# A hybrid decoder layer on one Trainium2 core: rounding each weight tile in a second, casting DMA

## The chip, the core and the metric

The kernel runs on one core of one Trainium2 chip. A core has five engines that work from queues of their own, each strictly in its order: TensorE (PE, matrix products; its weight loads are listed as PEld), VectorE (DVE), ScalarE (ACT), GpSimd (POOL) and SyncE (SP). They meet only through semaphores. Transfers between the chip's main memory and the on-chip memory are done by DMA engines; an instruction on SP or on POOL issues a transfer, and a semaphore tells when it has landed. The metric is the device time of one execution in microseconds (us). The kernel before took 613.98 us, the median of three runs that lie between 613.79 and 614.02.

## The reference

One decoder layer over 1024 tokens of width 1024, float32 throughout. Cut to what matters here:

```python
h = _rmsnorm(x, g_in[l])
proj = h @ w_in[l]                                   # 1024 x 3584
q_sb, k_sb, v_sb, u_c, b_c, c_c, q_mem, gate = jnp.split(proj, SPLIT_POINTS, axis=-1)
y_sb   = _stick_breaking_attention(q_sb, k_sb, v_sb)  # 8 heads of 64
y_conv = b_c * _causal_depthwise_conv(c_c * u_c, conv_w[l], conv_b[l])
mk, mv = jnp.split(_rmsnorm(mem, g_mem[l]) @ w_mem_kv[l], 2, axis=-1)
y_mem  = _memory_attention(q_mem, mk, mv)             # 4 heads of 64, 256 memory tokens
y = jnp.concatenate([_rmsnorm(y_sb), _rmsnorm(y_conv), _rmsnorm(y_mem)], axis=-1)
x = x + (y * jax.nn.silu(gate)) @ w_out[l]
return _rmsnorm(x, g_final)
```

In stick-breaking attention the weight of key s for query t is sigmoid(z_ts) times the product of (1 - sigmoid(z_tj)) over the keys j between s and t; the kernel computes these products as a running scan along the keys.

## The kernel before, in words

**Float32 from float32r.** A product of two float32 matrices is done as three TensorE passes on operands of type float32r. Each operand is split into hi, the value rounded to float32r, and lo, the exact rest: hi*hi + hi*lo + lo*hi. Each weight tile therefore needs three buffers: `raw` as loaded, `hi` and `lo`.

**Stages.** First the normalised input is split (`xh`, `xl`, eight tiles of each) and the values v are computed while the input still arrives. Then 24 tiles of the input projection (128 columns each, 512 KB) and four tiles of the memory's key and value weights (512 KB) are worked off one after the other by `proj`, `mem_kv` and, for the last one, `proj_last`. The order of these 28 is the string `BG`. A generator mixes them with the attention of twelve heads: the scores (z), two sigmoids on ACT (`F`, `sg`), the scan on DVE (lines 399 and 401), a product of `sg` and `F` on DVE or POOL (line 404, by the letters of `MENG`), transposes on TensorE, a split of the transposed weights (hi on ACT, line 341; lo on DVE, lines 342 and 344), and the product with v. POOL also sets the first column of each `F` tile (line 395) and adds up halves of y (line 361). Last comes the output projection: eight weight tiles of 512 KB, eight blocks of 128 rows, and the final norm.

**Weights.** `load_w` loads a tile on SP's queue into `wraw`, of which there is one buffer, rounds it in two halves to `whi` on ACT or DVE (by the 28 letters of `WENG`; lines 142 and 144), and subtracts on POOL to get `wlo` (line 145). There are two buffers each of `whi` and `wlo`: a tile can be made when the tile two before it has had its last matmul. `next_w` asks for a tile's successor as soon as the tile itself is taken into use. The output weights (`woh`, `wol`, lines 764 to 775) use the 16 buffers that `xh` and `xl` held, which fall free one after the other while `proj_last` runs; their rounding is on ACT (line 773), their subtraction on POOL for odd and on DVE for even tiles (line 774). Of their raw tiles `wor` there are three buffers.

**What sets the order.** The program is written through a scheduler that puts the instructions of each engine in an order by its own estimates of time. An edit at one place can thus move instructions everywhere. Once built, the order on each engine is fixed, and an instruction that waits holds up all that stand behind it on that engine. In the listings below, the buffer numbers are those of the built program.

Of the kernel before, what the change touches and what calls it, by code (L numbers as in the profile page):

```python
"""Hybrid decoder layer: stick-breaking attention, short gated convolution and memory
cross-attention heads side by side, group norms, SiLU gate, output projection.

The sequence is processed in reversed order (row j holds token T-1-j), so that the keys of a
query lie after it and the stick-breaking products are forward scans along the free axis:
  state[m] = max(state[m-1] * sigmoid(-z[m-1]), M[m]),   w[m] = sigmoid(z[m]) * state[m],
where M is one at the first key of the row and zero elsewhere.

Float32 products run as float32r passes: each operand is hi + lo, hi = the value rounded to
float32r, lo = the exact rest, and hi*hi + hi*lo + lo*hi carries float32's accuracy.  # L10
"""
# [16 lines left out]
T = 1024  # L28
# [16 lines left out]
# s, v, p: the engine (scalar, vector, pool) that rounds each weight tile, that takes each  # L45
# head's last product of the scan, and that splits its keys
WENG = 'vssssvvvsvvssvvsvvvssvvvvsss'
# [6 lines left out]
def hymba_kernel(ctx, tc, xT, xr, wp, wv, memT, memr, wmem, cols, eye, wout, gfin, out):  # L54
    nc = tc.nc
# [74 lines left out]
    nload = [0]  # L130

    def load_w(src, shape):
        hi = wring.tile(shape, F32R, tag="whi", name=nm("whi"))
        lo = wring.tile(shape, F32R, tag="wlo", name=nm("wlo"))
        raw = wring.tile(shape, F32, tag="wraw", name=nm("wraw"), bufs=1)
        nc.sync.dma_start(out=raw, in_=src)
        n = shape[1] // 2
        onact = WENG[nload[0]] == "s"
        nload[0] += 1
        for c in (slice(0, n), slice(n, 2 * n)):  # L140
            if onact:
                nc.scalar.copy(hi[:, c], raw[:, c])  # L142
            else:
                nc.vector.tensor_copy(hi[:, c], raw[:, c])  # L144
            nc.gpsimd.tensor_tensor(lo[:, c], raw[:, c], f(hi[:, c]), op=ALU.subtract)  # L145
        return hi, lo

# [11 lines left out]
    # the tensor engine's clock comes up on work: zeros, while the first rows load  # L159
# [82 lines left out]
    def behind_attention(ins):  # L242
        # order alone: keeps this work from running out ahead of the attention's steps
        if len(marks) > SLACK:
            tc.add_manual_dep(ins.ins, marks[-1 - SLACK].ins.name,
                              mybir.DependencyInfo(mybir.DependencyClass.NoSync, mybir.DependencyReason.DATA),
                              reason="pace")
# [3 lines left out]
    def proj_last(evac, need):  # L251
        # the input's tiles are done with one after the other: the output's weights take them
        wh, wl = next_w()
        ps = [z_tile(), z_tile()]
        for k in range(KC):
            for n, hf in enumerate(HALVES):
                for a, (ww, xx) in enumerate(((wh, xh), (wh, xl), (wl, xh))):
                    ins = nc.tensor.matmul(ps[n], lhsT=ww[:, k, :], rhs=xx[k][:, hf],
                                           start=(k == 0 and a == 0), stop=(k == KC - 1 and a == 2))
                    if a == 0:  # L260
                        behind_attention(ins)
            yield 1.3
        yield from after(need)
        for n, hf in enumerate(HALVES):
            evac(ps[n], hf)
# [65 lines left out]
    def transposed(blocks):  # L331
        # 4 [query, key] blocks: hi and lo of them; of a third and last one, lo comes after hi
# [21 lines left out]
    def put_own_key(y, av, a, t0):  # L354
        # one block of queries times their own keys: w's hi, then its lo
# [7 lines left out]
    def interleave(first, second):  # L363
        # steps of two lists of (cost, function), in proportion
# [89 lines left out]
    def stats_sum(st, g, first):  # L454
        # sums over the partitions, as a row, which a DMA lays out as [token, block]
        part = small.tile([P, TB], F32, tag="part", name=nm("part"), bufs=2)
        for n, (hi, lo) in enumerate(st["sq"]):
# [3 lines left out]
            row = stage()  # L461
# [8 lines left out]
    def group_stats(c):  # L470
        # the sums of squares of two tiles of 128 columns, a while later
# [222 lines left out]
    def attention(units):  # L694
        # steps of all heads in a row: the scores of a stage run one stage ahead of their use
# [16 lines left out]
    def run(steps, bg, ratio):  # L712
        # attention steps, with the other work in proportion
# [52 lines left out]
    for n, c in enumerate(order):  # L766
        hi = xpool.tile([P, D], F32R, tag="X", name=nm("woh"))
        lo = xpool.tile([P, D], F32R, tag="X", name=nm("wol"))
        raw = post.tile([P, D], F32, tag="wor", name=nm("wor"), bufs=3)
        nc.sync.dma_start(out=raw, in_=wout[c])  # L770
        eng = nc.gpsimd if n % 2 else nc.vector
        for hf in HALVES:
            nc.scalar.copy(hi[:, hf], raw[:, hf])
            eng.tensor_tensor(lo[:, hf], raw[:, hf], f(hi[:, hf]), op=ALU.subtract)  # L774
# [4 lines left out]
    for j in range(TB):  # L779
# [10 lines left out]
        # the last rows end on half a bank: less is left to do after the last product  # L790
# [78 lines left out]
```

## Time and profile before

| | |
|---|---|
| median of three runs | 613.98 us |
| profiled execution: its own time, and the span from its first to its last instruction | 614.2 us, 614.2 us |
| PE busy | 565.8 us, 92% |
| DVE busy | 454.3 us, 74% |
| ACT busy | 350.9 us, 57% |
| POOL busy | 338.7 us, 55% |
| moved by DMA | 48.36 MB, 79 GB/s on average |

A line of a timeline gives the start, the duration, the engine, the line of the kernel, the operation, what it writes and reads, the shapes and the count, and in brackets the idle time of that engine before it and what ended that. A line of a table of groups ends with the busy time of the group, the mean duration of one in ns, and the idle time before them by what ended it. A matmul's duration includes its way through the array; consecutive matmuls start closer together than they last, so a busy PE is not PE at its peak. The profile has no transfer issued by POOL in it: all 22,144 packets of the program's own transfers went through SP's queue.

### The profile page before, as it was taken

The numbers are of one execution on the slowest core, as the hardware profiler recorded it, in microseconds if no ns is written. First come the engines' busy times: TensorE is split into PE (matmuls) and PEld (weight loads), VectorE is DVE, ScalarE is ACT, GpSimd is POOL, SyncE is SP. The second block draws the span as 40 slices with busy tenths as digits, with TensorE's granted clock in tenths as the row PEclk, the third lists the DMA queues.
The fourth block names the chain that finished last, engine by engine and source line by source line (L and its number), as shares of the span: only waits on it lengthen the run. The fifth ranks groups of instructions, "written<-read, shape, count | busy, mean of one in ns | idle before, by whom it ended". The sixth has DMA issues, their size and how long they took to land.

```text
span 614.2 us, 8410 instructions
## 1 busy us (share of the span) xinstructions
PE 565.8 (92%) x2744; PEld 461.6 (75%) x2744; DVE 454.3 (74%) x744; ACT 350.9 (57%) x775; POOL 338.7 (55%) x381
## 2 busy tenths in 40 slices
PE   9999989979899899877979999899988999899995
PEld 5888878758678688755768888778667886688884
DVE  3425159989999996579966766998779668977664
ACT  5646556536685777765745988563645554443232
POOL 2551787454247448987858657448789668411001
PEclk9999999979999999898979999899999999999998
DMA  8931520211302021121313212111011163131311
GB/s 283 403 107 36 137 67 16 57 36 35 104 34 67 5 68 35 34 56 70 98 53 104 70 35 69 34 36 35 4 32 35 35 240 103 69 138 68 114 59 69
DMA packets 22188, 48.36 MB, mean 79 GB/s; under 512 B 7808, under 2 KB 8320, under 8 KB 22144
## 3 DMA queue, kind: packets, MB, share of 16 engines
q1 hardware_dynamic: 22144, 47.82, 24.3%
q8 instruction: 22, 0.36, 0.2%
q14 instruction: 22, 0.18, 0.1%
HBM read 36.78 MB, written 4.20 MB: 67 GB/s over the span
## 4 chain that ended last, share of the span: by engine, by line
DVE 17%; PE 16%; ACT 7%; issue 7%; POOL 6%; DMA 2%; POOLq 0%; DVEq 0%; ACTq 0%
PE tr L802 6%; PE pj L273 3%; PE pj L802 3%; PE z L802 2%; DVE wtl L342 2%; ACT e L546 2%; DVE F L401 2%; DVE F L399 2%; POOL wlo L145 2%; DMA wor<-in_wout 1%; DVE whi L144 1%; POOL sg L404 1%; DVE wol L774 1%; DVE mx L542 1%; DVE y L352 1%
## 5 line engine op out<-in xcount | busy, mean ns | idle before, releaser
L273 PE MATMUL pj<-xh,whi 128*128 128x512 f32 x368 | 150.1, 408 | 4.1 <-DVE mv L681 3.4
L273 PE MATMUL pj<-xl,whi 128*128 128x512 f32 x368 | 146.5, 398 | 0.0
L273 PE MATMUL pj<-xh,wlo 128*128 128x512 f32 x368 | 146.1, 397 | 0.0
L145 POOL TENSOR_TENSOR wlo<-wraw,whi 128x512 fp32r<-128x512 f32 x56 | 81.5, 1469 | 16.2 <-ACT whi L142 11.0
L399 DVE TENSOR_TENSOR_SCAN F<-F,mask 128x513 f32<-128x513 f32 (+2 forms) x64 | 78.8, 1231 | 13.7 <-ACT F L396 11.0
L273 PEld LDWEIGHTS pj<-xh,whi 128*128 128x128 f32 x368 | 70.8, 192 | 17.2 <-DVE mv L681 3.6
L273 PEld LDWEIGHTS pj<-xh,wlo 128*128 128x128 f32 x368 | 70.5, 192 | 14.3
L273 PEld LDWEIGHTS pj<-xl,whi 128*128 128x128 f32 x368 | 70.7, 192 | 12.2
L396 ACT ACTIVATE F<-z,nrq 128x512 f32<-128x512 f32 (+3 forms) x96 | 55.8, 583 | 22.8 <-PE z L389 11.0
L404 POOL TENSOR_TENSOR sg<-sg,F 128x512 f32<-128x512 f32 (+3 forms) x48 | 56.0, 1171 | 20.1 <-DVE F L401 10.3
L342 DVE TENSOR_TENSOR wtl<-tr,wth 128x512 fp32r<-128x512 f32 (+1 forms) x96 | 56.1, 592 | 11.0 <-ACT wth L341 10.1
L361 POOL TENSOR_TENSOR y<-y,avt 64x128 f32<-64x128 f32 x64 | 47.5, 743 | 22.8 <-DVE avt L359 20.1
L341 ACT CAST wth<-tr 128x512 fp32r<-128x512 f32 (+1 forms) x96 | 51.1, 553 | 14.3 <-PE tr L335 12.7
L397 ACT ACTIVATE sg<-z,rq 128x512 f32<-128x512 f32 (+2 forms) x96 | 55.4, 580 | 3.0 <-PE tr L335 2.8
L335 PE MATMUL tr<-ident,sg 128*128 128x128 f32 x288 | 48.4, 285 | 5.6 <-DVE stg L462 2.0
L401 DVE TENSOR_TENSOR_SCAN F<-F,F,mask 128x512 f32<-128x512 f32 (+1 forms) x32 | 43.9, 1371 | 7.6 <-ACT F L396 7.0
L395 POOL MEMSET F<- 128x1 f32 x96 | 8.9, 97 | 72.0 <-DVE F L401 35.8
L814 POOL TENSOR_TENSOR ssf<-ssf,nhalf 128x1 f32<-128x1 f32 x8 | 7.4, 924 | 71.4 <-DVE ssf L811 62.1
L316 POOL TENSOR_TENSOR qs<-qk,q 64x512 fp32r<-64x512 f32 x24 | 32.9, 1377 | 23.9 <-ACT q L315 23.2
L335 PEld LDWEIGHTS tr<-ident,sg 128*128 128x128 f32 x288 | 35.7, 147 | 10.6 <-DVE sg L404 3.1
L429 PE MATMUL av<-wtl,vh 128*128 128x256 f32 x128 | 35.5, 295 | 7.6 <-DVE wtl L342 7.4
L389 PE MATMUL z<-k,q 128*128 128x512 f32 (+2 forms) x96 | 36.2, 377 | 3.1 <-ACT sg L397 2.9
(188 smaller groups left out, 1283.2 us busy)
## 6 DMA issues: line engine op xcount, KB each, us to landing
wraw<-in_wp SPq DMA_DIRECT2D x24, 512.0 KB, 3.3
xs<-in_xr SPq DMA_DIRECT2D x8, 512.0 KB, 8.6
wor<-in_wout SPq DMA_DIRECT2D x8, 512.0 KB, 5.3
acc<-in_xr SPq DMA_DIRECT2D x8, 512.0 KB, 3.4
out<-acc SPq DMA_DIRECT2D x16, 256.0 KB, 2.1
xs<-in_xT SPq DMA_DIRECT2D x7, 512.0 KB, 8.0
qs<-q SPq DMA_DIRECT2D x12, 256.0 KB, 2.9
q<-qs SPq DMA_DIRECT2D x12, 256.0 KB, 2.9
```

Source lines behind the costliest of these rows:

```text
L145: nc.gpsimd.tensor_tensor(lo[:, c], raw[:, c], f(hi[:, c]), op=ALU.subtract)
L273: ins = nc.tensor.matmul(ps, lhsT=ww[:, k, :], rhs=xx[k][:, hf], start=(k == 0 and a == 0), stop=(k == KC - 1 and a == 2))
L335: ins = nc.tensor.transpose(tr[:, i * P : (i + 1) * P], blk, ident)
L341: nc.scalar.copy(wh[:, 0:n], tr[:, 0:n])
L342: nc.vector.tensor_tensor(wl[:, 0:m], tr[:, 0:m], f(wh[:, 0:m]), op=ALU.subtract)
L361: nc.gpsimd.tensor_tensor(y[own, t0 : t0 + P], y[own, t0 : t0 + P], c, op=ALU.add)
L396: nc.scalar.activation(F[:, 1:m], zz[:, 0 : m - 1], AF.Sigmoid, scale=nrq[:, i : i + 1])
L397: nc.scalar.activation(sg[:, c0:c1], zz, AF.Sigmoid, scale=rq[:, i : i + 1])
L399: nc.vector.tensor_tensor_scan(F[:, 0:m], F[:, 0:m], M[:, 0:m], 0.0, ALU.mult, ALU.max)
L401: nc.vector.tensor_tensor_scan(F[:, 0:m], F[:, 0:m], M[:, 130 : 130 + m], prev[:, H - lo : H - lo + 1], ALU.mult, ALU.max)
L404: eng.tensor_tensor(sg[:, c0:c1], sg[:, c0:c1], F[:, 0:w], op=ALU.mult)
L802: nc.tensor.matmul(ps[:, pc], lhsT=yy[:, c, :], rhs=ww[c][:, c0:c1], start=(c == cs[0] and a == 0), stop=(c == cs[-1] and a == 2))
```

## The change

Both places that make a hi tile, `load_w` and the loop over the output weights, now issue two transfers of the same source: one by POOL into the float32r tile, which rounds on the way (a casting DMA), and the former one by SP into `raw`. The copies on ACT and DVE that rounded are gone, and with them the table `WENG`. POOL's (or DVE's) subtraction now waits for both transfers. Comments were also taken out, so line numbers differ by up to 8: what was line 145 is line 137, line 404 is 396, line 774 is 766.

```diff
-WENG = 'vssssvvvsvvssvvsvvvssvvvvsss'
@@ load_w
         raw = wring.tile(shape, F32, tag="wraw", name=nm("wraw"), bufs=1)
+        nc.gpsimd.dma_start(out=hi, in_=src)
         nc.sync.dma_start(out=raw, in_=src)
         n = shape[1] // 2
-        onact = WENG[nload[0]] == "s"
-        nload[0] += 1
         for c in (slice(0, n), slice(n, 2 * n)):
-            if onact:
-                nc.scalar.copy(hi[:, c], raw[:, c])
-            else:
-                nc.vector.tensor_copy(hi[:, c], raw[:, c])
             nc.gpsimd.tensor_tensor(lo[:, c], raw[:, c], f(hi[:, c]), op=ALU.subtract)
@@ output weights
         raw = post.tile([P, D], F32, tag="wor", name=nm("wor"), bufs=3)
+        nc.gpsimd.dma_start(out=hi, in_=wout[c])
         nc.sync.dma_start(out=raw, in_=wout[c])
         eng = nc.gpsimd if n % 2 else nc.vector
         for hf in HALVES:
-            nc.scalar.copy(hi[:, hf], raw[:, hf])
             eng.tensor_tensor(lo[:, hf], raw[:, hf], f(hi[:, hf]), op=ALU.subtract)
```

Over the program DVE loses 30 instructions, ACT 42, and POOL gains 36 issues of transfers (28 for `whi`, 8 for `woh`). The order of the other instructions changes on every engine. Three places on POOL:

POOL's queue at the output weights before the change: `wol` is the subtraction of line 774, `stg` the last gates' products (line 588), `rg` a norm.

```order
L774 TENSOR_TENSOR wol_5256<-wor_5257,woh_5255 128x512 [waits DMAHW1_49,PE_49,Activation_49]
L588 TENSOR_TENSOR stg_5142<-stg_5142,stg_5143 128x512 [waits Activation_49]
L774 TENSOR_TENSOR wol_5272<-wor_5273,woh_5271 128x512 [waits DMAHW6_49,PE_49,Activation_49]
L588 TENSOR_TENSOR stg_5218<-stg_5218,stg_5219 128x512 [waits Activation_49,Pool_49]
L128 TENSOR_TENSOR rg<-rg,nhalf 128x8 [waits DVE_49]
L588 TENSOR_TENSOR stg_5224<-stg_5224,stg_5225 128x512 [waits Activation_49]
L774 TENSOR_TENSOR wol_5288<-wor_5289,woh_5287 128x512 [waits DMAHW0_49,PE_49,Activation_49]
L774 TENSOR_TENSOR wol_5304<-wor_5305,woh_5303 128x512 [waits DMAHW2_49,PE_49,Activation_49]
```

The same place with the change (line 762 issues the casting transfers, DMASW names their semaphores, line 766 is the subtraction; the second half of each subtraction is left out).

```order
L762 DMA woh_5226<-in_wout 128x1024 [waits PE_49]
L766 TENSOR_TENSOR wol_5227<-wor_5228,woh_5226 128x512 [waits DMAHW1_49,DMASW5_49,PE_49]
L762 DMA woh_5233<-in_wout 128x1024 [waits PE_49]
L580 TENSOR_TENSOR stg_5190<-stg_5190,stg_5191 128x512 [waits Activation_49]
L762 DMA woh_5240<-in_wout 128x1024
L766 TENSOR_TENSOR wol_5241<-wor_5242,woh_5240 128x512 [waits DMAHW6_49,DMASW7_49]
L762 DMA woh_5247<-in_wout 128x1024
L127 TENSOR_TENSOR rg<-rg,nhalf 128x8 [waits DVE_49]
L762 DMA woh_5254<-in_wout 128x1024
L766 TENSOR_TENSOR wol_5255<-wor_5256,woh_5254 128x512 [waits DMAHW0_49,DMASW1_49]
L762 DMA woh_5268<-in_wout 128x1024 [waits PE_49]
L766 TENSOR_TENSOR wol_5269<-wor_5270,woh_5268 128x512 [waits DMAHW2_49,DMASW3_49,PE_49]
```

Tiles 1, 3, 5 and 7 (5226, 5240, 5254, 5268) are issued and then waited for on the same queue, and the issues of tiles 2, 4 and 6 stand behind the waits of tiles 1, 3 and 5.

The start of POOL's queue, before the change and with it (`F` is line 395's column, `wsl` the subtraction of the values' weights).

```order
L864 UNCONDITIONAL_BRANCH [waits barrier_Pool_Activation_PE_DVE_SP_gather]
L395 MEMSET F_704 128x1
L395 MEMSET F_713 128x1
L395 MEMSET F_742 128x1
L189 ISA
L189 TENSOR_TENSOR wsl_135<-ws_133,wsh_134 128x512 [waits DMAHW1_49,DVE_49]
```

```order
L856 UNCONDITIONAL_BRANCH [waits barrier_Pool_Activation_PE_DVE_SP_gather]
L133 DMA whi_553<-in_wp 128x1024
L133 DMA whi_560<-in_wp 128x1024
L387 MEMSET F_701 128x1
L181 ISA
L181 TENSOR_TENSOR wsl_135<-ws_133,wsh_134 128x512 [waits DMAHW1_49,DVE_49]
```

The first two weight tiles' casting transfers, 512 KB each, wait for nothing and stand ahead of all other work.

POOL's queue around one tile in the middle of the program with the change (line 133 issues the casting transfer of a weight tile, line 137 is its subtraction).

```order
L133 DMA whi_4341<-in_wp 128x1024 [waits PE_49]
L353 TENSOR_TENSOR y_3945<-y_3945,avt_4215 64x128 [waits Pool_49]
L387 MEMSET F_4456 128x1 [waits DVE_49]
L137 TENSOR_TENSOR wlo_4342<-wraw_4343,whi_4341 128x512 [waits DMAHW2_49,DMASW7_49,PE_49]
L137 TENSOR_TENSOR wlo_4342<-wraw_4343,whi_4341 128x512
L440 TENSOR_TENSOR stg_4492<-stg_4492,stg_4493 128x512 [waits Activation_49]
```

Here an addition and a column are all that stands between the issue and the wait for what it issued.

More of the change, by code (lines that the diff above doesn't have):

```diff
@@ L128, in inv_rms @@
         nc.gpsimd.tensor_tensor(dst, dst, nhalf[:, 0:width], op=ALU.pow)
-    nload = [0]
     def load_w(src, shape):
```

## The prediction

> **What bounds the kernel now.** I read the page first: which engine is full, and which work makes up the chain that ended last.
>
> ```profile
> PE 565.8 (92%) x2744; PEld 461.6 (75%) x2744; DVE 454.3 (74%) x744; ACT 350.9 (57%) x775; POOL 338.7 (55%) x381
> DVE 17%; PE 16%; ACT 7%; issue 7%; POOL 6%; DMA 2%; POOLq 0%; DVEq 0%; ACTq 0%
> PE tr L802 6%; PE pj L273 3%; PE pj L802 3%; PE z L802 2%; DVE wtl L342 2%; ACT e L546 2%; DVE F L401 2%; DVE F L399 2%; POOL wlo L145 2%; DMA wor<-in_wout 1%; DVE whi L144 1%; POOL sg L404 1%; DVE wol L774 1%; DVE mx L542 1%; DVE y L352 1%
> ```
>
> TensorE is nearly full, and the time beyond its work is waiting. So next: the table of stretches (columns: the stretch in us, its length, busy time of PE, PEld, DVE, ACT and POOL, granted clock, DMA share, GB/s), and whom PE waited for.
>
> ```profile
> 5.00:84.00 79.00, 78.99 (x346) 64.73 (x346) 28.35 (x54) 46.25 (x91) 37.26 (x27) 1.00 0.54 187
> 84.00:280.00 196.00, 174.75 (x918) 146.12 (x917) 169.46 (x247) 126.02 (x260) 117.52 (x160) 0.96 0.17 49
> 280.00:312.00 32.00, 24.79 (x123) 20.13 (x123) 30.19 (x41) 19.73 (x45) 26.88 (x35) 0.87 0.23 67
> 312.00:420.00 108.00, 104.38 (x527) 86.73 (x526) 82.47 (x150) 74.98 (x169) 61.54 (x65) 0.96 0.19 54
> 420.00:450.00 30.00, 29.02 (x143) 22.55 (x142) 20.94 (x32) 13.99 (x28) 25.12 (x25) 1.00 0.13 36
> 450.00:497.00 47.00, 42.43 (x220) 34.95 (x220) 38.33 (x55) 27.01 (x65) 37.70 (x43) 1.00 0.16 49
> 533.00:598.00 65.00, 65.00 (x280) 52.29 (x279) 46.35 (x110) 23.70 (x81) 5.55 (x6) 1.00 0.26 89
> PE av L426 <- DVE wth L344: 10.8, 10, 2.1
> PE av L429 <- DVE wtl L342: 7.4, 5, 3.7
> PE pj L273 <- DVE mv L681: 3.4, 1, 3.4
> PE tr L802 <- DVE wol L774: 0.3, 1, 0.3
> ```
>
> Three things are to be seen. From 5 to 84 and from 533 to 598 PE never stands: a delay ahead of either stretch goes to the end in full. Between 84 and 497 PE stands for 413 - 375.4 = 37.6 us, mostly for the attention's splits on DVE. And no row has PE waiting for `whi` or `wlo`: weight tiles are early. How early, at the last of the 28 (ACT's rounding, begun when the tile two before let go of the buffer; POOL's subtraction; PE's first use):
>
> ```profile
> 489.64 1.14 ACT L142 CAST whi<-wraw 128x512 fp32r<-128x512 f32 x2 [2.54 <-PE pj L273]
> 490.40 2.55 POOL L145 TENSOR_TENSOR wlo<-wraw,whi 128x512 fp32r<-128x512 f32 x2 [0.55 <-ACT whi L142]
> 501.32 0.39 PE L258 MATMUL z<-xh,whi 128*128 128x512 f32 x1
> ```
>
> The buffer is free at about 489.6, `wlo` is done at 492.95, and PE comes at 501.3: 8.4 us to spare. The output weights are not early. There the row above (`tr` for `wol`, 0.3) is the tip of a chain of loads and subtractions that PE follows closely.
>
> **Part 1: what is taken away.**
>
> ```profile
> L144 DVE CAST whi<-wraw 128x512 fp32r<-128x512 f32 x30 | 26.0, 900 | 2.6 <-DMA wraw<-in_wp 2.6
> L142 ACT CAST whi<-wraw 128x512 fp32r<-128x512 f32 x26 | 14.8, 619 | 9.9 <-PE pj L273 9.4 <-DMA wraw<-in_wp 0.5
> L773 ACT CAST woh<-wor 128x512 fp32r<-128x512 f32 x16 | 9.1, 617 | 9.3 <-DMA wor<-in_wout 9.3
> L145 POOL TENSOR_TENSOR wlo<-wraw,whi 128x512 fp32r<-128x512 f32 x56 | 81.5, 1469 | 16.2 <-ACT whi L142 11.0 <-issue 1.9 <-DVE whi L144 1.8
> by line: issue 7.1%; PE tr L802 5.8%; PE pj L273 3.5%; PE pj L802 2.5%; PE z L802 2.5%; DVE wtl L342 2.3%; ACT e L546 1.8%; DVE F L401 1.7%; DVE F L399 1.7%; POOL wlo L145 1.6%; DMA wor<-in_wout 1.5%; DVE whi L144 1.4%; POOL sg L404 1.4%; D
> ```
>
> DVE loses 26.0 us of 454.3, ACT 23.9 of 350.9. Neither is full, so only the part that lies ahead of an attention step counts. In proportion, 26.0/454.3 = 5.7% of the 21.6 us in the three DVE rows of PE's waits is 1.2 us, and I add 0.8 for ACT: **-2.0**. The bounds are 0 and -8.6, the latter the 1.4% of the span for which `whi` of line 144 is itself on the chain (last row, the chain by line). I stay near the proportion, because the chain has other work of the same kind beside each cast.
>
> **Part 2: a transfer by POOL, its price.** No row shows one. The nearest are SP's transfers of the same size: in quiet stretches, over all eight output tiles, over those five issued between 500 and 535, and in the crowded start; the last row is SP's own time for an issue.
>
> ```profile
> wraw<-in_wp SPq DMA_DIRECT2D x24, 512.0 KB, 3.3
> wor<-in_wout SPq DMA_DIRECT2D x8, 512.0 KB, 5.3
> wor<-in_wout SPq DMA_DIRECT2D x5, 512.0 KB, 4.3
> xs<-in_xr SPq DMA_DIRECT2D x8, 512.0 KB, 8.6
> 509.39 0.33 SPq L770 DMA_DIRECT2D wor<-in_wout  x1
> ```
>
> I take L = 4.8 us from issue to landing, midway between 4.3 and 5.3, with the bounds 3.3 and 8.6, and 0.4 us of POOL's time for an issue. The Trainium skill ("DMA: Bandwidth & Descriptors", section "Anatomy of one DMA — SWDGE (gpsimd) path") fits a transfer issued by GpSimd as about 2.0 us plus the bytes over 436 GB/s. That is an estimate of 3.2 us for 512 KB; with it the sum below would be 619.6. No run here shows such a transfer yet.
>
> **Part 3: the start.** Two casting transfers, 1.05 MB, now go out first.
>
> ```profile
> GB/s 0 0 0 0 0 14 41 14 82 205 396 324 144 68 253 311 331 263 246 253 232 239 246 239 348 362 253 287 328 300 369 403 403 389 451 389 410 410 423 410
> 9.91 1.15 ACT L183 ACTIVATE xh<-xs,col 128x1024 fp32r<-128x1024 f32 x1 [0.66 <-DMA xs<-in_xT]
> 11.32 0.62 PE L199 MATMUL pj<-wsh,xh 128*128 128x512 f32 x2
> ```
>
> These are 40 slices of the first 12 us; from 3 us on the engines move 240 to 410 GB/s. The second input tile lands at 9.9 and is split at 11.06, just as PE takes it up (11.1 to 11.3): no slack. 1.05 MB at 410 GB/s is **+2.5 us** (0 if the transfers come late, 3.4 at 310 GB/s), and the stretch behind is full.
>
> **Part 4: the middle.** A `wlo` is now ready L + 2.55 = 7.35 us after its buffer is free, instead of 3.3: the 8.4 us to spare become 4.3, so PE's weights stay hidden (if not: 4 us a tile). What is not hidden is POOL's own queue. In the changed order zero to fifteen other instructions lie between issue and subtraction. Priced by POOL's group means (0.1 for a column, 0.74 for an addition to y, 1.4 for most others) they fall short of 4.8 us by 52 us in all over 26 tiles. POOL stood 16.2 us there before, so it stands 36 us more, and 28 issues add 11. Between 84 and 497 it has 413 - 268.8 = 144 us free, so it does not fill, but the columns of `F` and products `sg` behind each wait come late, and two stretches have little room (26.88 of 32, 25.12 of 30). PE stands 1.0 us in the second, so there is cover. **+2.5** (0 to +10). The stall of 3.4 us for `mv` I leave:
>
> ```profile
> 300.21 3.37 POOL L145 TENSOR_TENSOR wlo<-wraw,whi 128x512 fp32r<-128x512 f32 x2
> 307.75 2.30 DVE L144 CAST whi<-wraw 128x512 fp32r<-128x512 f32 x2 [1.74 <-DMA wraw<-in_wp]
> 310.32 2.50 POOL L145 TENSOR_TENSOR wlo<-wraw,whi 128x512 fp32r<-128x512 f32 x2
> ```
>
> DVE's cast ahead of `mv` goes, but POOL is without a pause until 310.3 and PE wants this `wlo` a microsecond later: 0.
>
> **Part 5: the output weights.**
>
> ```profile
> 505.79 1.30 POOL L451 TENSOR_TENSOR stg<-stg,stg 128x512 fp32r<-128x512 f32 x1 [0.73 <-ACT stg L450]
> 507.36 1.45 POOL L588 TENSOR_TENSOR stg<-stg,stg 128x512 f32<-128x512 f32 x1 [0.27 <-ACT stg L587]
> 515.67 2.84 POOL L774 TENSOR_TENSOR wol<-wor,woh 128x512 fp32r<-128x512 f32 x2 [1.76 <-ACT woh L773]
> 520.07 1.65 POOL L128 TENSOR_TENSOR rg<-rg,nhalf 128x8 f32<-128x8 f32 x1 [0.31 <-DVE rg L127]
> 528.38 2.99 POOL L774 TENSOR_TENSOR wol<-wor,woh 128x512 fp32r<-128x512 f32 x2 [1.82 <-ACT woh L773]
> 537.85 0.93 PE pj L802 x4
> 538.79 2.80 PE tr L802 x12
> ```
>
> Before, POOL's last `wol` ends at 531.4. Now tiles 1, 3, 5 and 7 are fetched and awaited in turn. Tile 1 is issued behind the stats at 507.1 and subtracted by 507.1 + 4.8 + 2.8 = 514.7. Issue 2, two gate products (1.3 each) and then tile 3: issued 517.7, done 525.3. Issue 4, `rg` 1.65, tile 5: issued 527.4, done 535.0. Issue 6, tile 7: issued 535.4, done 543.0. That is four times L, so each us of L counts four. PE then needs 0.9 us for its last products of row 0 and 24 matmuls at 65/280 = 0.23 us for row 1: both rows are done at 549.5. Before, they were done when the twelve of the last row-1 group ended at 541.6, less the four of row 2 among them: 540.7. **+8.8** (2.8 at L = 3.3, 24.0 at 8.6); all behind it is the full stretch.
>
> **Sum.** 614.2 (the profiled execution's span and its own time; the median is 613.98, 0.2 less) + 2.5 - 2.0 + 2.5 + 8.8 = 626.0, so I say 626.
>
> **Rivals.** *The relief wins* (faster). All 8.6 us of casts on the chain go, landings are as quick as 3.3, and the start hides: 614.2 - 8.6 + 2.8 = 608.4, or 610.9 with the start. For it: DVE is the largest share of the chain. Against it: the output weights' queue, which no cast relieves. *The landings come late.* One mechanism: POOL's issue is held up by DVE. For it: the subtraction takes 2.55 us alone but 3.37 at 300.2, where DVE is busy without a break. At L = 6.7 the end costs 16.4, the middle 26 x 1.9 = 49 us more of standing on POOL, which I price at +8: 614.2 + 2.5 - 2 + 8 + 16.4 = 639. From L = 8.5 the middle's standing passes POOL's 144 free us, and it becomes the bound: 650 and more. The Trainium skill ("SBUF — State Buffer", section "SBUF: two separate sides") says that GpSimd cannot write a transfer's descriptors while VectorE runs an operation in two-port mode, such as an fp32 copy. The change itself takes out 30 such casts, so that rule alone gives little. *The transfers are hidden.* L = 3.3, start absorbed: 614.2 + 2.8 + 2.5 - 2 - 1.5 of `mv` = 616.
>
> **Chances.** Forecast 47% (620 to 633), late landings 22% (633 to 650), hidden 17% (613 to 620), relief 14% (under 613). A fifth of a per cent (1.2 us) is about what a measurement here can tell from no change. A third of the hidden case lies within it: faster 14%, same 6%, slower 80%. The range of 8 in 10 takes in the hidden case and most of the late one, 612 to 643.
>
> **What would show it.** Right: POOL's second largest idle time is before `wlo` and `wol`, ended by a DMA; `wol` of tile 7 ends some 11 us later against `proj_last`'s end; PE stands about 9 us in the first two rows of the output projection; PE's second input tile comes 2 to 3 us later. Wrong: a landing under 3.5 us, or PE's waits for `wth` and `wtl` down by more than 5 us.

## The result, and the profile after

The changed kernel took 632.55 us (median of four runs, 628.61 to 632.87) against 613.88 for the kernel before beside it: a ratio of 1.0297, with a 95% interval of 1.0252 to 1.0342. It is slower, by 18.7 us; the forecast was 626 us, 12 us slower. For the sums below one thing must be known: in all later comparisons a kernel's time lies 1.7 to 2.0 us above its span (the kernel before: 614.37 with a span of 612.5), so the page of before, with a span of 614.2, is of an execution some 1.6 us longer than the median, and a difference of two traces understates that of the medians by about as much. Executions of one kernel spread widely (18 of the kernel before: 610.9 to 617.4), so a few microseconds between two single traces say little by themselves.

The page of the changed kernel: the engines, the chain that ended last by engine and by line, and the transfers (KB each, median us from issue to landing).

```profile
PE 570.7 (90%) x2744; PEld 464.2 (74%) x2744; DVE 441.9 (70%) x714; ACT 329.0 (52%) x733; POOL 353.9 (56%) x417
PE 41%; DVE 26%; issue 9%; POOL 9%; DMA 6%; ACT 6%; SPq 2%; POOLq 0%; DVEq 0%; ACTq 0%
PE pj L265 15%; PE tr L794 5%; DVE F L391 5%; DVE F L393 4%; DVE wtl L334 3%; DVE sg L396 3%; DMA woh<-in_wout 3%; PE pj L794 2%; PE av L421 2%; PE z L794 2%; PE tr L327 2%; DVE y L582 2%; PE z L191 2%; PE pj L191 2%; PE tr L191 2%
whi<-in_wp POOLq DMA_DIRECT2D x24, 512.0 KB, 3.7
woh<-in_wout POOLq DMA_DIRECT2D x8, 512.0 KB, 4.0
```

ACT's busy time fell by 21.9 us, about its copies. DVE's fell by 12.4 only, though 26.0 us of copies are gone: its products of `sg` and `F`, 48 as before, took 31.7 us (663 ns each), and now

```profile
L396 DVE TENSOR_TENSOR sg<-sg,F 128x512 f32<-128x512 f32 (+3 forms) x48 | 40.3, 842 | 2.3
```

DVE's relief is thus half of what was taken away: with the copies gone its products are slower (the last section shows beside what). DMA is 6% of the chain. The chain's shares on the page of before can't be set beside these: they add up to 55%, because that chain reaches back only to 270.4 us. A casting transfer lands 3.7 to 4.0 us after its issue.

Where the time went, from three places of the traces, PE's last product of the values, of the input projection, and the 96th of the output projection (the first two rows): before 49.6, 513.4 and 540.7 us; after 54.6, 519.4 and 557.1; behind that the two run alike. So **the start costs 5.0 us, the middle 1.0, the end 10.4**. The end first, as the table of stretches shows it from the last product of the input projection to the 96th of the output projection (columns as in the prediction): before the change, and after.

```profile
513.35:540.65 27.30, 24.14 (x97) 17.56 (x97) 24.05 (x40) 11.44 (x29) 14.28 (x11) 1.00 0.24 78
```

```profile
519.38:557.08 37.70, 29.18 (x98) 20.19 (x97) 24.09 (x42) 5.95 (x19) 18.81 (x18) 0.86 0.45 141
```

The same 97 products take 27.3 and 37.7 us. Of the 10.4, PE stands 5.4 longer (27.30 - 24.14 = 3.2, then 8.5). The other 5.0 it is busy longer with the same work, at a granted clock of 0.86 where it had 1.00. This is how PE spends the 10.4 us; what makes them is the chain.

Rows of the chain of the changed kernel in that stretch (start, length, what).

```profile
510.08 3.48 DMA woh<-in_wout
526.90 4.05 DMA woh<-in_wout
531.03 2.44 POOL wol L766 x2
535.74 4.33 DMA woh<-in_wout
540.15 2.51 POOL wol L766 x2
543.18 4.27 DMA woh<-in_wout
547.58 2.52 POOL wol L766 x2
551.22 3.06 PE tr L794 x12
```

This is Part 5's picture: issue, landing, subtraction, and only then the next issue. (The first row is tile 0, the others are tiles 3, 5 and 7.) POOL's last `wol` ends at 550.1, that is 30.7 us behind the input projection (18.0 before). From tile 3's issue at 526.9 to 551.2 no row of the chain is PE's. PE's slow clock therefore lies beside the chain here. PE takes up the last half of tile 7 at 550.2, as soon as it is there; at full clock it would only have stood longer (an inference from the chain, no run shows it). Whom the chain holds up, from the table of PE's waits:

```profile
PE tr L794 <- DMA woh<-in_wout: 4.2, 2, 2.4
PE z L794 <- POOL wol L766: 1.1, 2, 0.6
```

Mostly PE does not even get as far as `wol`: it waits for `woh` itself (tiles 4 and 6), whose issue stood behind the wait for another tile.

The start, on PE's timeline of the changed kernel (behind eight products on zeros), with POOL's row for the first two issues.

```profile
1.25 1.25 POOL L133 DMA_DIRECT2D whi<-in_wp  x2 [0.79 <-POOLq L852]
6.69 0.80 PE L191 MATMUL pj<-wsh,xh 128*128 128x512 f32 x1 [1.83 <-ACT xh L175]
9.81 1.05 PE L191 MATMUL pj<-wsh,xl 128*128 128x512 f32 x2
10.66 1.05 PE L191 MATMUL z<-wsh,xh 128*128 128x512 f32 x2
14.05 0.62 PE L191 MATMUL av<-wsh,xh 128*128 128x512 f32 x2
14.51 0.63 PE L191 MATMUL tr<-wsl,xh 128*128 128x512 f32 x2
```

The same place before:

```profile
4.69 1.45 PE L199 MATMUL pj<-wsh,xh 128*128 128x512 f32 x2
6.74 0.63 PE L199 MATMUL pj<-wsl,xh 128*128 128x512 f32 x2
7.21 0.62 PE L199 MATMUL z<-wsl,xh 128*128 128x512 f32 x2
```

Two products start 0.85 us after the two before them from 9.8 until about 13.9 us in the changed kernel, 0.46 later on, and 0.46 from 6.7 us on before the change. So the first real product is 2.0 us late, and the first tile then takes 3.0 us longer, most of it at half the rate.

### The profile page after: what moved, and what is told of

The parts are those of the page before. It is cut to its first block, busy times and chain, and to the rows that moved or that the text cites. A ratio compares the mean times of both kernels' runs of the same rounds, so it can differ in the third digit from the quotient of the medians.

```text
span 630.8 us, 8340 instructions
## 1 busy us (share of the span) xinstructions
PE 570.7 (90%) x2744; PEld 464.2 (74%) x2744; DVE 441.9 (70%) x714; ACT 329.0 (52%) x733; POOL 353.9 (56%) x417
## 4 chain that ended last, share of the span: by engine, by line
PE 41%; DVE 26%; issue 9%; POOL 9%; DMA 6%; ACT 6%; SPq 2%; POOLq 0%; DVEq 0%; ACTq 0%
PE pj L265 15%; PE tr L794 5%; DVE F L391 5%; DVE F L393 4%; DVE wtl L334 3%; DVE sg L396 3%; DMA woh<-in_wout 3%; PE pj L794 2%; PE av L421 2%; PE z L794 2%; PE tr L327 2%; DVE y L582 2%; PE z L191 2%; PE pj L191 2%; PE tr L191 2%
## 5 line engine op out<-in xcount | busy, mean ns | idle before, releaser
L137 POOL TENSOR_TENSOR wlo<-wraw,whi 128x512 fp32r<-128x512 f32 x56 | 86.9, 1572 | 22.8 <-issue 7.0
L391 DVE TENSOR_TENSOR_SCAN F<-F,mask 128x513 f32<-128x513 f32 (+2 forms) x64 | 76.6, 1201 | 23.5 <-ACT F L388 17.7
L265 PEld LDWEIGHTS pj<-xh,whi 128*128 128x128 f32 x368 | 70.1, 190 | 13.9 <-DVE stg L578 1.8
L333 ACT CAST wth<-tr 128x512 fp32r<-128x512 f32 (+1 forms) x96 | 51.2, 554 | 17.1 <-PE tr L327 16.2
L353 POOL TENSOR_TENSOR y<-y,avt 64x128 f32<-64x128 f32 x64 | 41.6, 650 | 21.9 <-DVE avt L351 19.7
L327 PE MATMUL tr<-ident,sg 128*128 128x128 f32 x288 | 49.2, 285 | 3.3 <-DVE sg L396 2.1
L421 PE MATMUL av<-wtl,vh 128*128 128x256 f32 x128 | 36.8, 303 | 12.7 <-DVE wtl L334 12.7
L396 DVE TENSOR_TENSOR sg<-sg,F 128x512 f32<-128x512 f32 (+3 forms) x48 | 40.3, 842 | 2.3
L421 PE MATMUL av<-wth,vh 128*128 128x256 f32 x128 | 38.4, 305 | 0.6 <-ACT wth L333 0.6
```

The source lines that it names most:

```text
L265: ins = nc.tensor.matmul(ps, lhsT=ww[:, k, :], rhs=xx[k][:, hf], start=(k == 0 and a == 0), stop=(k == KC - 1 and a == 2))
L327: ins = nc.tensor.transpose(tr[:, i * P : (i + 1) * P], blk, ident)
L333: nc.scalar.copy(wh[:, 0:n], tr[:, 0:n])
L391: nc.vector.tensor_tensor_scan(F[:, 0:m], F[:, 0:m], M[:, 0:m], 0.0, ALU.mult, ALU.max)
L396: eng.tensor_tensor(sg[:, c0:c1], sg[:, c0:c1], F[:, 0:w], op=ALU.mult)
L421: nc.tensor.matmul(av, lhsT=key(j), rhs=w[:, c], start=(g == 0 and n == 0), stop=(g == ng - 1 and j == (g == 0) and n == 1))
```

## The experiments

The difference is to the kernel before beside each run (613.9 to 614.8 us); the interval is of the ratio.

| run | us | ratio (95%) | difference |
|---|---|---|---|
| the change | 632.55 | 1.0297 (1.0252 to 1.0342) | +18.7 |
| 1: load_w alone | 621.94 | 1.0130 (1.0084 to 1.0176) | +7.6 |
| 2: output weights alone | 628.67 | 1.0240 (1.0192 to 1.0288) | +14.3 |
| 3: more products on zeros | 630.22 | 1.0261 (1.0215 to 1.0307) | +15.9 |
| 4: first two tiles by engines | 627.82 | 1.0220 (1.0172 to 1.0267) | +13.5 |
| 5: load_w alone, from the third tile | 618.11 | 1.0061 (1.0039 to 1.0084) | +3.3 |
| 6: output weights issued ahead | 628.65 | 1.0236 (1.0195 to 1.0276) | +13.8 |
| 7: transfer and copy | 627.86 | 1.0219 (1.0181 to 1.0257) | +13.0 |
| 8: neither transfer nor copy | 607.14 | 0.9888 (0.9854 to 0.9923) | -7.7 |
| 9: output rest on DVE | 627.88 | 1.0207 (1.0180 to 1.0233) | +13.5 |
| 10: before, other letters | 613.78 | 0.9985 (0.9967 to 1.0002) | -0.6 |
| 11: a transfer nobody waits for | 617.86 | 1.0057 (1.0027 to 1.0088) | +3.5 |
| 12: before, all copies on ACT | 609.93 | 0.9921 (0.9899 to 0.9943) | -4.4 |

By the medians the 18.7 us are 5.2 for the first two transfers (the change less run 4), 10.2 for those of the output weights (run 4 less run 5) and 3.3 for the rest (run 5). Each of the first two is a difference of two runs, and uncertain by some 3 to 4 us. The 3.3 are not the middle alone: behind the input projection runs 1 and 5 need 28.3 and 29.3 us to the 96th product, where the kernel before needs 27.3, so the middle's own net is some 1 to 3 us.

**Run 1: load_w alone.** The output weights are rounded by ACT again.

```diff
-        nc.gpsimd.dma_start(out=hi, in_=wout[c])
         nc.sync.dma_start(out=raw, in_=wout[c])
         for hf in HALVES:
+            nc.scalar.copy(hi[:, hf], raw[:, hf])
             eng.tensor_tensor(lo[:, hf], raw[:, hf], f(hi[:, hf]), op=ALU.subtract)
```

> Casting transfers in load_w alone; the output weights are rounded by ACT as before. The theory (three separate places: the start cost 5.0 us, the middle 1.0, the output weights' queue on POOL 10.4, and 1.7 lie outside the span): the order up to the output weights is that of the changed kernel, so PE's last matmul of the input projection ends at about 519.4 as there, and the 10.4 of the end are gone: 620.5 to 623. The rival (the output weights are late because transfers crowd one another, whoever waits for them): their second, plain transfers alone would come little sooner, and it stays at 627 or more.

Measured 621.94, as the theory said. Up to the output weights this kernel's order is that of the changed kernel, and from there to the 96th product it takes 28.3 us, one more than before.

**Run 2: the output weights alone.** The kernel before, with the changed loop over the output weights.

> The kernel before, with casting transfers for the output weights alone. The theory: all up to 513 us is as before, and the in-turn waits on POOL cost four times issue to landing (about 4 us each, less what POOL's 1.76 and 1.82 us of waiting for ACT were before): the 96th matmul of the output projection comes 8 to 11 us later, total 622 to 626 (the upper end if the 1.7 us outside the span belong to any POOL transfer). The rival (the end of the changed kernel is slow because of what the middle hands on): 617 or less.

Measured 628.67, above the 622 to 626 expected: in this order the end costs 14.7 us, not 10.4. The groups of `wol` in this run (busy, mean ns | idle time before them and what ended it):

```profile
L774 POOL TENSOR_TENSOR wol<-wor,woh 128x512 fp32r<-128x512 f32 x8 | 10.9, 1374 | 18.2 <-DMA woh<-in_wout 11.3 <-PE z L258 3.6 <-PE pj L802 3.2
L774 DVE TENSOR_TENSOR wol<-wor,woh 128x512 fp32r<-128x512 f32 x8 | 6.9, 907 | 11.1 <-DMA woh<-in_wout 11.1
```

POOL stands 18.2 us before its four subtractions and DVE 11.1 before its own, mostly for landings. The loss belongs to these eight transfers: all of it is there with the middle of the kernel before.

**Run 3: more products on zeros.** `WARM = 14` in place of 8 in the changed kernel.

> The changed kernel with 14 instead of 8 matmuls on zeros ahead of the first real one. Theory A (of the 5.0 us lost at the start 2 are late data and 3 are a low clock, because PE stood 1.8 us between the last of the eight and the first real matmul): PE does not stand there, the first tile's 24 matmuls run 0.23 us apart, the values end at 51.5 to 52.5 instead of 54.6, total 629.5 to 630.5. Theory B (all 5.0 are late data): the values end at 54.6 or later and the total stays at 632 to 633.

The trace agrees with theory A: the values end at 52.0 instead of 54.6. The time is 2.3 us less, which by itself is within the two intervals. The row of PE where the first real product starts:

```profile
7.02 0.50 PE L191 MATMUL pj<-wsh,xh 128*128 128x512 f32 x1 [0.41 <-ACT xh L175]
9.21 0.63 PE L191 MATMUL pj<-wsh,xl 128*128 128x512 f32 x2
9.68 0.62 PE L191 MATMUL z<-wsh,xh 128*128 128x512 f32 x2
```

The data come as late as in the changed kernel, but PE stood only 0.41 us, and the pairs of products are 0.46 apart from the first: the first tile takes 6.9 us, not 9.8.

**Run 4: the first two tiles by engines.** The changed kernel, but DVE rounds the first weight tile and ACT the second, as before.

```diff
+        nload[0] += 1
+        if nload[0] > 2:
             nc.gpsimd.dma_start(out=hi, in_=src)
```

> The changed kernel, but the first two weight tiles are rounded by DVE and ACT as in the kernel before, so that no casting transfer lies in the start. The theory (those two transfers delay the first input pieces by 2 us, and the rest follows from that): the values end at 49.6 as before, 5.0 sooner, and if the middle keeps its loss the total is 626.5 to 628.5. The rival (the start is slower because of POOL's or ACT's new order): the values end at 53 or later, total 631 to 633.

Measured 627.82, and the values end at 49.2. The whole loss of the start comes from these two transfers: 2 us by their bytes ahead of the first input pieces, and up to 3 by the clock, of which run 3 gives back 2.6. That second part is not the same in every execution: with the same two transfers the values end at 54.6 in the changed kernel, 54.1 and 54.5 in runs 1 and 9, but 53.0 and 52.6 in runs 6 and 7.

**Run 5: load_w alone, from the third tile on.** Run 4 with the output weights rounded by ACT.

> Casting transfers in load_w from the third tile on; the first two tiles and the output weights are rounded by engines as in the kernel before. The theory (the loss has two places, start and output weights; between them the change itself gains): the order is that of the run with the first two tiles rounded by engines, up to the output weights, so the input projection ends at about 511.0 (513.35 before the change), the end is that of the run with load_w alone (95.3 us from there, 94.6 before): 1.0 to 2.5 us less than the kernel before, ratio 0.996 to 0.999. The rival (that gain of 2.4 us was the clock of one execution, or transfers cost elsewhere): ratio 1.001 or more.

I had read a gain of 2.4 us in the middle out of one trace of run 4; measured is a loss of 3.3 in all. The rival holds: that gain lay within what two single traces differ by. (Run 5's own trace, 2.1 us under its median, has the middle 1.6 us shorter than the trace of before and the end 2.0 longer.) So the middle's net is small, and I asked what it is the net of (runs 7, 8 and 11).

**Run 6: the output weights issued ahead.** All eight casting transfers in a loop of their own, ahead of the subtractions.

```diff
+    his = [xpool.tile([P, D], F32R, tag="X", name=nm("woh")) for _ in order]
     for n, c in enumerate(order):
         ...
+        nc.gpsimd.dma_start(out=his[n], in_=wout[c])
+    for n, c in enumerate(order):
```

> The changed kernel, but the eight casting transfers of the output weights are issued in a loop of their own ahead of all their subtractions. The theory (it is the issues of tiles 2, 4, 6 and 7 behind the waits of 1, 3 and 5 that make the end late): the 96th matmul of the output projection comes within 2 us of where it comes when ACT rounds (28.3 us after the input projection, against 37.7 in the changed kernel), and the total is 621 to 624. The rival (twice the bytes in these 30 us are too many): 628 or more, with PE still waiting for landings of woh.

Measured 628.65. The theory of the in-turn waits fails here as the whole cause: PE no longer waits for any `woh`, and yet from the input projection to the 96th product it takes 36.4 us. The rival's time came, but not by its reason. The stretch, the landings, and PE's longest waits in it:

```profile
516.69:553.13 36.44, 28.49 (x99) 20.18 (x98) 29.13 (x44) 6.54 (x21) 18.89 (x13) 0.86 0.34 121
woh<-in_wout POOLq DMA_DIRECT2D x8, 512.0 KB, 6.9
wor<-in_wout SPq DMA_DIRECT2D x8, 512.0 KB, 5.9
PE z L795 <- DVE acc L797: 3.3, 2, 3.0
PE tr L795 <- DVE stg L454: 3.1, 2, 1.9
```

Both kinds of transfer now land 2 to 3 us later than in the changed kernel (4.0 and 4.0 there); POOL's eight are all issued within 9 us. So the rival's crowding is there, though no wait of PE ends with a landing. PE stands 8.0 us, nearly all for several things on DVE, and it is busy for 28.5 us at a clock of 0.86 instead of 24.1; in this run products of PE stand on the chain as well.

**Run 7: transfer and copy.** The kernel before with the casting transfer into `whi` in front, and the copies kept.

```diff
+        nc.gpsimd.dma_start(out=hi, in_=src)
         nc.sync.dma_start(out=raw, in_=src)
```

> The kernel before, with the casting transfer into whi in front and the copies kept: load_w issues both transfers, waits for both, and then rounds into whi as before; nothing is taken away. Output weights as before. By the prediction's terms, start 5.0 as measured plus 2.5 for POOL's waits in the middle: 620.5 to 623, of which 2 to 4 between 84 and 505 us. The rival (the middle of the changed kernel is only another order and the waits cost nothing there): 618.5 to 620.

Measured 627.86, far above both. The start costs 3.0 here and the middle 9.5 by the trace (the medians' 13.0 less 3.0 is 10). The `wlo` group of this run, and DVE's copies:

```profile
L146 POOL TENSOR_TENSOR wlo<-wraw,whi 128x512 fp32r<-128x512 f32 x56 | 81.9, 1479 | 27.5 <-DVE whi L145 17.9 <-ACT whi L143 8.7 <-PE av L430 0.6
L145 DVE CAST whi<-wraw 128x512 fp32r<-128x512 f32 x30 | 17.3, 618 | 7.0 <-DMA whi<-in_wp 4.5 <-PE tr L461 1.9 <-issue 0.6
```

POOL stands 11 us more before `wlo` than the 16.2 of before. DVE and ACT now stand for landings as well (4.5 and 3.8 us), which the changed kernel does not have; so I take 10 us as an upper price for the transfers. It is no strict bound: DVE's copies also got 8.7 us shorter here (17.3 instead of 26.0).

**Run 8: neither transfer nor copy.** The kernel before; from the third tile on only one column of 128 is still rounded.

```diff
+        w = slice(0, shape[2] if nload[0] < 3 else 1)
-                nc.scalar.copy(hi[:, c], raw[:, c])
+                nc.scalar.copy(hi[:, c, w], raw[:, c, w])
         ...    # DVE's copy likewise; hi is one of two fixed buffers
```

> The kernel before, without the rounding of the weight tiles from the third on: whi keeps what the first two tiles left in it (one column of 128 is still rounded), wlo is computed from that, and no casting transfer is made. The result therefore is not the layer's; the time is that of the relief alone. By the prediction's term the relief is worth 2.0 us: 611.5 to 613. The rival from the record (all 8.6 us of casts on the chain go): 605 to 607. The rival that order alone decides: anything within 3 us of before, slower too.

Measured 607.14: the copies are worth 7.7 us (4.7 to 9.0 by the interval), almost the largest figure on record, though small copies remain (DVE's take 14.3 us instead of 26.0, ACT's 5.8 instead of 14.8). PE's largest wait in the middle is down to

```profile
PE av L430 <- DVE wth L348: 7.8, 6, 2.3
```

where before the change the two largest, both for splits on DVE, were 10.8 and 7.4.

**Run 9: the output rest on DVE.** The changed kernel with all subtractions of output tiles on DVE (`eng = nc.vector`); POOL waits for no landing of an output tile.

> The changed kernel, but all eight output tiles are subtracted on DVE, so that POOL issues their casting transfers and waits for none of them. The theory (POOL's waits in turn hold back the next issues): from the input projection's end to the last matmul it is 96 to 99 us (104.9 in the changed kernel, 95.3 where ACT rounds the output weights), total 622 to 626. The rival (each landing is late anyway, or DVE with ten more microseconds of work takes POOL's place): 629 or more.

Measured 627.88, between the theory's 622 to 626 and the rival's 629. From the input projection to the last product it takes 102.0 us, not 96 to 99. To the 96th product it takes 35.0 us against 37.7: by the traces only 2.7 of the 10.4 come back. By the medians it is 4.7 us for the whole kernel, nearer half. POOL's queue:

```profile
533.88 1.66 POOL L127 TENSOR_TENSOR rg<-rg,nhalf 128x8 f32<-128x8 f32 x1 [3.19 <-DVE rg L126]
535.51 1.66 POOL L762 DMA_DIRECT2D woh<-in_wout  x3
```

The issues now stand behind the gates' products and the norm, each of which waits for another engine. An issue on a queue that computes is held by whatever waits there, not by `wol` alone. And other things take POOL's place on the chain: two late landings, the second of a `raw` tile, and products of PE, most of them at half the rate.

```profile
520.65 5.57 DMA woh<-in_wout
526.36 3.49 PE z L794 x6
529.84 4.16 PE pj L794 x12
537.60 6.98 DMA wor<-in_wout
```

These 18 products took 7.7 us; at 0.23 us apart, as before the change, they would be an estimated 4.2. Here the clock does cost time.

**Run 10: other letters.** The kernel before with `WENG` moved on by one place.

> The kernel before with the 28 letters of WENG moved on by one place: as many tiles are rounded on ACT and on DVE as before, but other ones, and so the scheduler's order is another. Nothing is added or taken away. It shows what another order alone does. If the measured terms of the middle (7.7 us for the copies, about 10 for the transfers) are the work's own: within 3 us of the kernel before. If the order alone moves the time by as much as these terms: 5 us or more away, on either side.

Measured 613.78, within 1 us of before: this other order alone does not make a difference of 3 to 10 us. It is one order; others were not tried, and at the output weights the same transfers took 42.0 us in run 2's order, 37.7 in that of the change.

**Run 11: a transfer nobody waits for.** The kernel before, with a transfer of `wlo` to a spare place in main memory behind each subtraction from the third tile on. It has the size of a casting transfer, but goes the other way.

```diff
+        if nload[0] > 2:
+            spare = dram.tile(shape, F32R, name=nm("spare"))
+            nc.gpsimd.dma_start(out=spare, in_=lo)
```

> The kernel before, and POOL issues from the third weight tile on one more transfer of the same size and kind (wlo to a spare place in main memory) right behind the subtraction that makes wlo, for which nobody waits but the buffer's next use. If the middle's loss beside the transfers is the waiting for them (the theory): 614 to 618, since 26 issues of 0.6 us and the traffic lie beside other work. If POOL's time for the issues, or the traffic, is what costs: 621 or more.

Measured 617.86, +3.5 us, at the upper end of the theory's range. POOL's time for the issues:

```profile
L148 POOL DMA_DIRECT2D spare<-wlo x26 | 15.6, 601 | 0.9 <-POOL wlo L145 0.6
```

So 26 issues of 0.6 us and 13.6 MB of traffic cost 3.5 us (1.7 to 5.4 by the interval) where nobody stands for them. If run 7's 10 us are the price of the whole, waiting is up to 6.5 of it.

**Run 12: all copies on ACT.** The kernel before with `WENG` all `s`.

> The kernel before with all 28 weight tiles rounded on ACT: DVE is relieved of its 30 copies (26.0 us) without any second transfer, ACT gets 30 more (18.6 us). If it is DVE's copies that hold up the attention (the theory for most of the 7.7 us that the run without copies gained): 607 to 612. If ACT's copies hold it up as much: 614 or more.

Measured 609.93, as the theory said: quicker than both kernels, than the one before by 0.8%. ACT's copies and POOL's subtractions in this run:

```profile
L142 ACT CAST whi<-wraw 128x512 fp32r<-128x512 f32 x56 | 32.0, 623 | 13.5 <-PE pj L273 11.1 <-DMA wraw<-in_wp 2.3
L145 POOL TENSOR_TENSOR wlo<-wraw,whi 128x512 fp32r<-128x512 f32 x56 | 75.0, 1355 | 16.2 <-ACT whi L142 15.8
```

DVE is rid of 26.0 us, ACT has 17.2 more, and POOL needs 6.5 us less for the same subtractions (81.5 before). More than half of run 8's relief can be had without any second transfer. How much of the 4.4 us is DVE's and how much POOL's was not separated.

## Why the prediction was right and wrong

The direction, and the largest term, were right: slower, most of it at the output weights, by transfers fetched and awaited in turn on POOL. 632.55 lies within the range of 612 to 643 and at the edge of the forecast's own 620 to 633. The 6.5 us that are missing are mis-sized terms: by the medians 2.7 at the start, about 1.4 at the end, and the rest in the net of the middle, where two larger errors happened to cancel.

**Part 2, the price.** L was set at 4.8 us; measured 3.7 and 4.0. An issue was set at 0.4 us of POOL's time; measured 0.6. The estimate of 3.2 from the Trainium skill ("DMA: Bandwidth & Descriptors", section "Anatomy of one DMA — SWDGE (gpsimd) path") is below every median of a casting transfer seen here (3.6 to 6.9), though for the weight tiles' 3.7 it is nearer than my 4.8. Its sum of 619.6 would have been further off, because the other terms were too small.

**Part 3, the start: +2.5, measured 5.0 (5.2 by the medians).** The transfers' bytes were right: the first input pieces, 64 to 256 KB, land 2.6 to 2.9 us later (5.3 to 6.1 us after issue instead of 2.7 to 3.3). (The 240 to 410 GB/s that I read off the row of rates hold from about 4.2 us on, not from 3.) Two things were not right. The place: not the second input tile is late (its split ends 1.2 us later), but the first pieces, by 2.0 us at PE. And the step left out what PE's standing does to its clock: up to 3.0 us more, of which run 3 gives back 2.6. "PE's second input tile comes 2 to 3 us later" was therefore wrong.

**Part 1, the relief: -2.0, measured -7.7 (run 8).** "In proportion" failed. A share of DVE's busy time says little where an engine works in order: a copy can delay all that stands behind it. Run 12, which gains 4.4 us by moving DVE's 30 copies away, fits that, but no run follows a single copy's delay. The bound of 8.6 was near by luck. It is the copies' share of a chain whose first row is this:

```profile
270.40 0.01 POOL F L395
```

The copies of the first 270 us are not in it, so it bounds nothing.

**Part 4, the middle: +2.5, measured up to 10 (run 7), of which 3.5 without any waiting (run 11).** PE's weights stayed hidden, as said: PE waits 0.4 us for a `wlo` in all. But POOL's standing, from which the step was worked out, did not come: before `wlo` it stood 22.8 us where it had stood 16.2, so 6.6 more and not 36. Only 3.2 of the 22.8 ended with a landing of `whi`. With the measured L of 3.7 the step's own sum, 52 less 26 times 1.1, gives about 7 more. POOL stands instead ahead of the issues, mostly until PE lets go of the buffer (8.9 us in this row, 3.3 for the memory's four tiles):

```profile
L133 POOL DMA_DIRECT2D whi<-in_wp x24 | 14.4, 600 | 8.9 <-PE pj L265 8.0 <-POOLq L852 0.8
```

By what way the transfers cost the middle its 10 us is therefore open. That they make `F` and `sg` late, as the step said, is not shown; PE's waits for splits on DVE did not fall but rose.

```profile
PE av L421 <- DVE wtl L334: 12.7, 6, 7.5
PE av L418 <- DVE wth L336: 11.0, 7, 2.9
```

They were 7.4 and 10.8. Two errors of some 6 and 7 us thus nearly cancelled, which was luck: the net of Parts 1 and 4 was said to be +0.5 and is some +1 to +3. The change takes away a real cost and puts a slightly larger one in its place.

**Part 5, the end: +8.8, measured 10.4 (10.2 by the medians).** This step was right as a mechanism. It put POOL's last subtraction 29.7 us behind the input projection (543.0 less 513.3) and the 96th product 6.5 us behind that; measured are 30.7 and 7.0. The chain shows the landings one behind the other, 3.5 to 4.3 us each. That the sum fits so well is partly luck: the shorter L was made up for by waits the step did not have (a gate's product stands 1.6 us for ACT ahead of tile 3's issue, and another 2.0 ahead of the first subtraction) and by issues of 0.6. PE stands 8.5 us in that stretch, 5.4 more than before; its slow clock fills the rest of the time and is not on the chain. But taking POOL's turn-taking away does not take the loss away: with POOL's waits gone (run 9) or the issues made early (run 6), 2.7 and 1.3 us of the 10.4 come back by the traces, and the whole kernel is 4.7 and 3.9 us quicker by the medians. In run 9's chain late landings and PE's slow clock take over. What one thing would bring PE's 27.3 us back, with casting transfers kept, is open; no run found it.

**The rivals.** "The transfers are hidden" and "the relief wins" fell with the whole change, but the relief was real. "Landings come late" asked for L of 6.7; the medians in the changed kernel are 3.7 and 4.0. Of what was to show the forecast wrong, the waits for `wth` and `wtl` did not go down. Single landings of `woh` came just under 3.5 us (the chain's first row has 3.48), the medians did not. Of what was to show it right, one did not come: POOL's longest idle times are before `ssf` and `F`, for DVE, as they were; 11.2 us before `wol` ended with a landing, and 3.2 before `wlo`.

## What to carry to other kernels

A transfer that costs an engine nothing still has to be issued: on a queue that also computes and waits, each issue is late by whatever waits ahead of it, so look at that queue before the transfer's duration. Where a full TensorE is made to stand for about 2 us, ask what its clock then costs, and whether PE is on the chain there: at the start of the changed kernel it added up to 3 us to 2, at the end it lay beside the chain. And do not price a relief by the engine's busy share; leave the work out once and measure, then try the cheap form of it: moving the copies to the emptier engine gained 4.4 us where the transfer lost 18.7. Before a share of the chain is used as a bound, see how far back the chain reaches.

## What the runs showed of the hardware beyond that

**Short stands cost clock.** On PE's timeline of the changed kernel, in the output projection:

```profile
538.96 0.71 PE L794 MATMUL tr<-woh,yh 128*128 128x512 f32 x2 [1.81 <-DMA woh<-in_wout]
540.15 0.63 PE L794 MATMUL tr<-woh,yl 128*128 128x512 f32 x1
540.58 0.63 PE L794 MATMUL tr<-wol,yh 128*128 128x512 f32 x1
```

Behind a stand of 1.81 us products start 0.43 us apart instead of 0.23, until 542.7; the same behind the next stand, of 2.42. The stretches to both sides of the point where the granted clock falls (columns as in the prediction):

```profile
536.24:539.65 3.41, 1.60 (x7) 0.73 (x5) 1.84 (x4) 0.00 (x0) 0.09 (x1) 1.00 0.85 302
539.65:543.06 3.41, 3.41 (x9) 2.70 (x9) 0.49 (x1) 0.00 (x0) 2.91 (x3) 0.50 0.49 154
```

In all fourteen traces the slow spells behind the start lie on such a grid of 3.41 us, one to three steps each. A step at full clock with less than 1.5 us of PE's work was always followed by a slow one, a step with more than 2.0 never. So it is the sum of PE's standing in a step that counts, and not one long stand. The Trainium skill ("TensorE: Matmul & The Clock Gate", section "What's actually happening") gives half rate after an idle window of about 3.4 us and full rate after as long a busy one. The half rate and the length of a slow spell agree; here a step with 1.6 us of work already counted as idle.

**POOL and DVE lengthen each other's work.** The copies of the kernel before, with the shortest, the median and the longest in ns:

```profile
L144 DVE CAST whi<-wraw x30: 407/648/2760, 19.9 to 436.9; 128x512 fp32r<-128x512 f32 x30
```

Sorted in the traces by what runs beside them, the two of these copies with no TENSOR_TENSOR of POOL beside them took 0.42 us, the other 28 took 0.94 on average (in run 7, with the same copies, 10 took 0.42 and 20 took 0.72). A 128x512 product of `sg` and `F` on DVE took 0.69 us alone in both kernels; beside POOL it took 1.03 before (7 of 20) and 1.39 with the change (10 of 20). POOL's subtraction took 1.29 us with DVE idle, in every trace. The split `wtl` took 0.68 either way, so not all of DVE's work is touched. Much of DVE's relief went that way: of the 13.6 us by which its busy time did not fall (26.0 less 12.4), these products took 8.6. The Trainium skill ("SBUF — State Buffer", section "SBUF: two separate sides") says that GpSimd and certain VectorE operations, an fp32 copy among them, lock each other out of a shared port; the copies' 0.42 and 0.94 us agree.

Over all its subtractions POOL's mean was 1469 ns before, 1355 with all copies on ACT (run 12) and 1464 in run 11. In the changed kernel, whose DVE makes no copies either, it is larger:

```profile
L137 POOL TENSOR_TENSOR wlo<-wraw,whi 128x512 fp32r<-128x512 f32 x56 | 86.9, 1572 | 22.8 <-issue 7.0 <-PE z L381 5.5 <-PE tr L327 3.5
```

The copies are not what lengthens it: before the change the 13 subtractions beside a copy took 1474 ns, the 43 others 1467. Those beside a scan took longer than the others (1646 and 1355 before, 1794 and 1439 with the change). Why the same number of scans cost more in the changed kernel was not settled.
